# Second selection over 80 candidate sums instead of 256, and one table block issued ahead of the gate products

## The chip, the cores and the metric

The kernel runs on one core of one Trainium2 chip. The metric is the device time of one execution in microseconds (us); smaller is better. Each engine of the core has its own instruction queue: PE (TensorE, matrix products; PEld is its weight load), DVE (VectorE), ACT (ScalarE), POOL (GpSimd) and SP (SyncE, which here only issues loads). A queue is served in order.

## What is computed

The reference runs two transformer-like blocks over 256 tokens of width 1024. The change lies in the retrieval layer of the first block. For every token and each of 8 heads it scores 128 + 128 sub-keys, keeps the best 16 of each half, adds them pairwise, and keeps the best 16 of the 256 sums; the chosen pairs address 128 x 128 experts.

```python
s = jnp.einsum('thpk,hpnk->thpn', q, sub_keys)
sv, si = lax.top_k(s, P_TOPK)                                  # 16 of 128, two halves
cand = (sv[:, :, 0, :, None] + sv[:, :, 1, None, :]).reshape(TOKEN_BLOCK, P_HEADS, 256)
cidx = (si[:, :, 0, :, None] * N_KEYS + si[:, :, 1, None, :]).reshape(TOKEN_BLOCK, P_HEADS, 256)
fv, fpos = lax.top_k(cand, P_TOPK)                             # 16 of 256
eidx = jnp.take_along_axis(cidx, fpos, axis=-1)
g = jax.nn.softmax(fv, axis=-1)
u = u_tab[eidx]
act = jax.nn.gelu(jnp.einsum('td,thkd->thk', xb, u))
return jnp.einsum('thk,thkd->td', g * act, v_tab[eidx])
```

## The kernel before

**Every expert is computed.** The kernel does not gather rows. It multiplies all tokens by all 128 blocks of `peer_u` (128 experts each, function `U(b)`), applies gelu, multiplies by a gate matrix that is zero for experts not chosen, and multiplies by all 128 blocks of `peer_v`. One such block is 24 matrix products of 128x128 by 128x256: every weight is split into a high and a low part (`whi` by ACT, line 109; `wlo` by DVE, line 117), and `mm3` (lines 160 to 162) adds high-high, high-low and low-high. `fill` makes these parts ahead of their use, `wlo` three units ahead of the one that is issued, in the order of a fixed list of units; the raw weights come two units per load from SP (line 93), into three buffers, each free when both its units' `wlo` are made. A unit's product lands in one of two PSUM banks (`m`), which ACT empties (gelu at line 790, or a copy of a query at line 841).

**Selection, lines 806 to 850.** For head 0 to 7 the queue order is two query units, a table block, the eight score products (line 810), another table block. `tick` advances generators between units. Generator `topk` has three steps: the score products; `top16` over 128 scores, twice for each of two token halves (`tt`); the sums `cand` (line 825) and `top16` over them. `top16` (lines 308 to 319) is `max` (8 best), `max_index`, `match_replace`, `max`, `max_index`; the profile shows each `max_index` and `match_replace` as two instructions, a short MATCH_VALUE_LOAD and the pass itself. Its instructions alternate between the two halves. One head's sums are selected one unit after its scores are.

**Decoding, lines 857 to 911 (`finish`).** The position 0 to 255 of a chosen sum is split into its two ranks by a shift and a mask (lines 867, 868) and converted (line 870). Then come the softmax over the 16 (`g`, `gz`), transposes on PE (lines 881, 889), and 16 passes that turn ranks into key numbers (line 903). Two table blocks are issued between the first part of `finish` and the transposes.

**Gates, lines 923 to 976.** Loop `og` runs 32 times over 8 tokens each: DVE makes one-hot matrices `o` and `go` (lines 950, 951) one turn ahead, PE multiplies them (16 gate products, line 969), ACT copies the result into `stg` (line 972), and every second turn `stg` is written to a DRAM tensor `gd` (line 974, issued on ACT's queue). Each turn ends with one table block, as long as more than seven are left. After the loop seven blocks remain. The gates are read back as `gt` (line 990), `w_mult` (line 1000, DVE) multiplies them into the activations, `w_hi` (line 1007, ACT) and `w_lo` (line 1012, DVE) split them, and the products with `peer_v` begin. ACT's `w_hi` for blocks 0 to 2 stands in its queue between the gelus of the last blocks.

Of the kernel before, what the change touches and what calls it, by code (L numbers as in the profile page):

```python
# [13 lines left out]
F32 = mybir.dt.float32  # L14
# [6 lines left out]
OP = mybir.AluOpType  # L21
# [14 lines left out]
UKEEP = 7  # L36
# [29 lines left out]
class Kx:  # L66
# [692 lines left out]
    def peer(self):  # L759
        nc, tc, a = self.nc, self.tc, self.a  # L760
# [26 lines left out]
        def U(b):  # L787
            p = self.unit("peer_u", b, h)
            acts[b] = t = actp.tile([128, T], F32, name="act")
            nc.scalar.activation(t, p, AF.Gelu)  # L790

        pre = deque(range(2, NPRE))
        with c2:
            pkt = c2a.enter_context(tc.tile_pool(name="pkt", bufs=2))
            sx = [pk.tile([128, 8, 2, 16], U32, name=f"sx{i}") for i in range(2)]
            fx = [pk.tile([128, 8, 16], U32, name=f"fx{i}") for i in range(2)]
# [9 lines left out]
            def topk(hd, qp):  # L806
                ps = [self.side(), self.side()]
                for tt in range(2):
                    for i in range(2):
                        nc.tensor.matmul(ps[tt][:, i * 128:(i + 1) * 128], qp[:, i, tt * 128:(tt + 1) * 128],  # L810
                                         keys[:, 2 * hd + i], start=i == 0, stop=True, skip_group_check=True)
                yield
                sv_ = [pkt.tile([128, 2, 16], F32, name=f"sv{i}") for i in range(2)]
                grp = []
                for tt in range(2):
                    for i in range(2):
                        w = pkt.tile([128, 128], F32, name=f"tkw{tt}{i}", bufs=1)
                        grp.append((ps[tt][:, i * 128:(i + 1) * 128], w, sv_[tt][:, i], sx[tt][:, hd, i]))
                self.top16(grp)
                yield  # L820
                grp = []
                for tt in range(2):
                    cd = pkt.tile([128, 16, 16], F32, name=f"cand{tt}", bufs=1)
                    sv = sv_[tt]
                    nc.vector.tensor_tensor(cd, sv[:, 0, :, None].to_broadcast([128, 16, 16]),
                                            sv[:, 1, None, :].to_broadcast([128, 16, 16]), op=OP.add)
                    cf = cd.rearrange("p a b -> p (a b)")
                    w = pkt.tile([128, 256], F32, name=f"cw{tt}", bufs=1)
                    grp.append((cf, w, fv[tt][:, hd], fx[tt][:, hd]))
                self.top16(grp)  # L830

            self.tasks.append(topk(0, qp0))
            for hd in range(1, 8):
                qp = pkt.tile([128, 2, T], F32, name="qp", bufs=2)
# [4 lines left out]
                for i in range(2 if hd > 1 else 0):  # L839
                    p = self.unit("w_query", 2 * hd + i, h)  # L840
# [12 lines left out]
            pft = c2.enter_context(tc.tile_pool(name="pft", bufs=2))  # L853
# [3 lines left out]
            def finish():  # L857
                g = [pf_.tile([128, 8, 16], F32, name=f"g{tt}") for tt in range(2)]
                pf = [pf_.tile([128, 2, 8, 16], F32, name=f"pf{tt}") for tt in range(2)]
                sxf = [pf_.tile([128, 2, 8, 16], F32, name=f"sxf{tt}") for tt in range(2)]  # L860
                for tt in range(2):
                    v = fv[tt]
                    nc.vector.tensor_tensor(g[tt], v, v[:, :, 0:1].to_broadcast([128, 8, 16]), op=OP.subtract)
                    nc.scalar.activation(g[tt], g[tt], AF.Exp)
                for tt in range(2):
                    pi = pft.tile([128, 2, 8, 16], U32, name="pi")
                    nc.vector.tensor_scalar(pi[:, 0], fx[tt], 4, None, op0=OP.logical_shift_right)
                    nc.vector.tensor_scalar(pi[:, 1], fx[tt], 15, None, op0=OP.bitwise_and)
                    nc.vector.tensor_copy(sxf[tt].rearrange("p s h a -> p h s a"), sx[tt])
                    nc.vector.tensor_copy(pf[tt], pi)  # L870
                for tt in range(2):
                    gz = pft.tile([128, 8], F32, name="gz")
                    nc.vector.tensor_reduce(gz, g[tt], axis=AX.X, op=OP.add)
                    nc.vector.reciprocal(gz, gz)
                    nc.vector.tensor_tensor(g[tt], g[tt], gz[:, :, None].to_broadcast([128, 8, 16]), op=OP.mult)
                for _ in range(FW):
                    yield
                for tt in range(2):
                    p = self.side()
                    for j, src in enumerate((sxf[tt][:, 0], sxf[tt][:, 1], pf[tt][:, 0], pf[tt][:, 1])):  # L880
                        nc.tensor.transpose(p[:, j * 128:(j + 1) * 128], src.rearrange("p a b -> p (a b)"),
                                            self.ident)
                    ts = slice(tt * 128, (tt + 1) * 128)
                    p = p.rearrange("p (k s t) -> p k s t", k=2, s=2)
                    nc.scalar.copy(sxT[:, :, ts], p[:, 0])
                    nc.scalar.copy(posT[:, :, ts], p[:, 1])
                p = self.side()
                for tt in range(2):
                    nc.tensor.transpose(p[:, tt * 128:(tt + 1) * 128], g[tt].rearrange("p a b -> p (a b)"),
                                        self.ident)  # L890
                slot = pf_.tile([128, T], F32, name="slot")
                nc.scalar.mul(slot, p[:, :T], GSCALE)
                yield
                acc = self.bank(0)
                last = None
                for a0 in range(0, 16, FA):
                    cur = []
                    for a in range(a0, a0 + FA):
                        pb = self.side()
                        nc.tensor.matmul(pb, pick[:, a].rearrange("p h w -> p (h w)"),  # L900
                                         sxT.rearrange("p s t -> p (s t)"), start=True, stop=True)
                        t = pft.tile([128, 2 * T], BF, name="hit", bufs=2 * FA)
                        nc.vector.scalar_tensor_tensor(t, posT.rearrange("p s t -> p (s t)"), float(a), pb,
                                                       op0=OP.is_equal, op1=OP.mult)
                        cur.append((a, t))
                    yield
                    for a, t in cur:
                        nc.tensor.matmul(acc, identb, t, start=a == 0, stop=a == 15)
                nc.scalar.copy(ib.rearrange("p t j -> p j t"), acc.rearrange("p (j t) -> p j t", j=2))
                nc.vector.tensor_copy(gp[:, :, 0], slot)  # L910
                nc.vector.tensor_tensor(gp[:, :, 1], slot, gp[:, :, 0], op=OP.subtract)

            self.side_cycle = ("s", "s", "a1", "a2")
            self.tasks.append(finish())
            while self.tasks:
                self.tick()
# [6 lines left out]
        with ExitStack() as c3:  # L923
# [35 lines left out]
            for og in range(T // OG):  # L959
                o2, go = nxt  # L960
                if og + 1 < T // OG:
                    nxt = onehots(og + 1)
                if og % (TG // OG) == 0:
                    stg = pgt.tile([128, 128, TG], F32, name="stg")
                for q in range(OG // 4):
                    p = self.side().rearrange("p (t i) -> p t i", t=4)
                    for i in range(4):
                        for j in range(2):
                            nc.tensor.matmul(p[:, i], o2[:, q * 4 + i], go[:, q * 4 + i, j],  # L969
                                             start=i == 0 and j == 0, stop=j == 1, skip_group_check=True)  # L970
                    e0 = (og % (TG // OG)) * OG + q * 4
                    nc.scalar.mul(stg[:, :, e0:e0 + 4].rearrange("p i t -> p t i"), p, 1.0 / GSCALE)  # L972
                if og % (TG // OG) == TG // OG - 1:
                    nc.scalar.dma_start(gd[:, og * OG // TG], stg)
                if len(pre) > UKEEP:
                    U(pre.popleft())

        c1.close()
        banks = [self.bank(i) for i in range(4)]
# [607 lines left out]
```

## Time and profile before

| | |
|---|---|
| median of 3 runs | 1481.99 us (1478.51 to 1486.52) |
| profiled execution, its own time | 1480.42 us |
| its span, first to last instruction | 1478.7 us |
| PE busy | 1380.0 us, 93% |
| DVE busy | 1116.5 us, 76% |
| ACT busy | 767.0 us, 52% |

The profiled execution's time is 1.72 us more than its span, and 1.57 us less than the median. Busy shares are means over stages that have different limits; stages are told apart by windows of time, in us from the span's start.

### The profile page before, as it was taken

How to read it: one execution, taken by the hardware profiler on the slowest of the kernel's cores; microseconds unless marked ns; L12 is line 12 of the kernel's file. 1: busy time of each engine (PE TensorE's matmuls, PEld its weight loads, DVE VectorE, ACT ScalarE, POOL GpSimd, SP SyncE). 2: the span in 40 equal slices, each digit the busy share in tenths (PEclk: the TensorE clock that was granted, in tenths of full speed). 3: DMA queues.
4: the chain of work that ended last, by engine and by line, in shares of the span. 5: the costliest groups of instructions: out<-in, count | busy, mean ns of one | idle time of the engine just before them, and what ended most of it. 6: DMA issues, size and time to landing. Idle time of an engine off the chain costs nothing.

```text
span 1478.7 us, 27412 instructions
## 1 busy us (share of the span) xinstructions
PE 1380.0 (93%) x11208; PEld 1332.7 (90%) x11208; DVE 1116.5 (76%) x2066; ACT 767.0 (52%) x1241; POOL 119.3 (8%) x95
## 2 busy tenths in 40 slices
PE   3898988979999999999999999999979899899997
PEld 2777887978899999999999999999979789899997
DVE  7887789996799677777777766666789968765554
ACT  3545654424699754444445444444555485553442
POOL 0020020000000000000000000000148530100000
PEclk8999999998999999999999999999999999999999
DMA  9556543444577888888888867666445325445451
GB/s 378 188 202 211 199 158 115 146 141 143 180 279 283 291 313 294 311 309 310 285 291 312 303 214 243 221 235 211 148 141 170 132 99 198 144 160 197 172 189 68
DMA packets 106062, 317.31 MB, mean 215 GB/s; under 512 B 5584, under 2 KB 34640, under 8 KB 103632
## 3 DMA queue, kind: packets, MB, share of 16 engines
q1 hardware_dynamic: 65696, 250.54, 48.7%
q10 hardware_dynamic: 39408, 61.87, 11.8%
q0 software_dynamic: 832, 3.15, 0.6%
q8 instruction: 88, 1.44, 0.4%
q14 instruction: 38, 0.31, 0.1%
HBM read 297.71 MB, written 17.83 MB: 213 GB/s over the span
## 4 chain that ended last, share of the span: by engine, by line
PE 70%; DVE 23%; ACT 4%; issue 1%; DMA 1%; POOL 0%; DVEq 0%; POOLq 0%; SPq 0%; ACTq 0%
PE m L160 11%; PE m L161 11%; PE m L162 11%; PE a L161 11%; PE a L160 11%; PE a L162 11%; DVE wlo L117 5%; DVE a L1149 3%; PE s L969 2%; DVE junk L323 1%; DMA raw<-in_ada_w 1%; ACT whi L109 1%; DVE cacc L553 1%; DVE score L1108 1%; DVE mdt L291 1%
## 5 line engine op out<-in xcount | busy, mean ns | idle before, releaser
L160 PE MATMUL m<-hi,whi 128*128 128x256 f32 x1816 | 522.6, 288 | 10.3 <-DVE cacc L553 4.1
L117 DVE TENSOR_TENSOR wlo<-raw,whi 128x1024 fp32r<-128x1024 f32 x398 | 480.8, 1224 | 56.0 <-ACT whi L109 45.8
L162 PE MATMUL m<-hi,wlo 128*128 128x256 f32 x1816 | 513.2, 283 | 8.8 <-DVE wlo L117 8.7
L161 PE MATMUL m<-lo,whi 128*128 128x256 f32 x1816 | 513.0, 282 | 0.0
L109 ACT CAST whi<-raw 128x1024 fp32r<-128x1024 f32 x428 | 444.8, 1046 | 61.5 <-DMA raw<-in_peer_v 27.1
L160 PEld LDWEIGHTS m<-hi,whi 128*128 128x128 f32 x1816 | 347.4, 191 | 13.5 <-issue 4.3
L162 PEld LDWEIGHTS m<-hi,wlo 128*128 128x128 f32 x1816 | 346.4, 191 | 10.2 <-DVE wlo L117 9.9
L161 PEld LDWEIGHTS m<-lo,whi 128*128 128x128 f32 x1816 | 347.2, 191 | 0.6
L162 PE MATMUL a<-wh,wlo 128*128 128x256 f32 x1024 | 288.2, 281 | 0.0
L161 PE MATMUL a<-wl,whi 128*128 128x256 f32 x1024 | 288.2, 281 | 0.0
L160 PE MATMUL a<-wh,whi 128*128 128x256 f32 x1024 | 287.9, 281 | 0.0
L162 PEld LDWEIGHTS a<-wh,wlo 128*128 128x128 f32 x1024 | 192.9, 188 | 0.0
L161 PEld LDWEIGHTS a<-wl,whi 128*128 128x128 f32 x1024 | 192.7, 188 | 0.0
L160 PEld LDWEIGHTS a<-wh,whi 128*128 128x128 f32 x1024 | 192.6, 188 | 0.0
L1012 DVE TENSOR_TENSOR wl<-act,wh 128x256 fp32r<-128x256 f32 x128 | 54.5, 426 | 137.7 <-PE a L161 122.9
L790 ACT ACTIVATE act<-m 128x256 f32<-128x256 f32 x126 | 48.4, 384 | 165.4 <-PE m L162 165.4
L1007 ACT CAST wh<-act 128x256 fp32r<-128x256 f32 x128 | 51.9, 406 | 143.6 <-DVE act L1000 121.2
L323 DVE SCALAR_TENSOR_TENSOR junk<-mraw,silu 128x1024 bf16<-128x1024 f32 x80 | 97.6, 1220 | 7.2 <-DMA mraw<-in_ada_w 7.0
L117 POOL TENSOR_TENSOR wlo<-raw,whi 128x1024 fp32r<-128x1024 f32 x33 | 79.2, 2421 | 41.7 <-ACT whi L109 35.2
L972 ACT ACTIVATE stg<-s 128x512 f32<-128x512 f32 x64 | 64.6, 1119 | 3.3 <-PE s L969 3.2
L1000 DVE TENSOR_TENSOR act<-act,gt 128x256 f32<-128x256 f32 x128 | 53.7, 419 | 5.0 <-DMA gt<-gd 5.0
L161 PE MATMUL a<-fl,whi 128*128 128x256 f32 x176 | 49.8, 283 | 0.1
(438 smaller groups left out, 1801.8 us busy)
## 6 DMA issues: line engine op xcount, KB each, us to landing
raw<-in_peer_u SPq DMA_DIRECT2D x64, 1024.0 KB, 5.8
raw<-in_peer_v SPq DMA_DIRECT2D x64, 1024.0 KB, 5.1
mraw<-in_w_ada ACTq DMA_DIRECT2D x48, 512.0 KB, 5.5
raw<-in_w_ffn_in SPq DMA_DIRECT2D x22, 1024.0 KB, 5.1
gd<-stg ACTq DMA_DIRECT2D x16, 1024.0 KB, 6.9
gt<-gd ACTq DMA_DIRECT2D x14, 1024.0 KB, 8.0
mraw<-in_ada_w SPq DMA_DIRECT2D x24, 512.0 KB, 4.6
raw<-in_w_ffn_out SPq DMA_DIRECT2D x11, 1024.0 KB, 5.0
```

The lines of the kernel that those rows point to most:

```text
L109: self.nc.scalar.copy(t, self.raw[k])
L117: eng.tensor_tensor(t, self.raw.pop(k), h.bitcast(F32), op=OP.subtract)
L160: mm(out, w[0], x[0], start=start, stop=False, **kw)
L161: mm(out, w[0], x[1], start=False, stop=False, **kw)
L162: mm(out, w[1], x[0], start=False, stop=stop, **kw)
L323: self.nc.vector.scalar_tensor_tensor(junk, w, 0.5, self.silu_c[i], op0=OP.mult, op1=OP.mult, accum_out=self.mod[i][:, u:u + 1])
L790: nc.scalar.activation(t, p, AF.Gelu)
L972: nc.scalar.mul(stg[:, :, e0:e0 + 4].rearrange("p i t -> p t i"), p, 1.0 / GSCALE)
L1000: nc.vector.tensor_tensor(tv, tv, gv, op=OP.mult)
L1007: nc.scalar.copy(wts[b], acts[b])
L1012: nc.vector.tensor_tensor(wl, acts.pop(b), wts[b].bitcast(F32), op=OP.subtract)
L1149: nc.vector.scalar_tensor_tensor(zp, z[:, c, k:k + T], w, zp, op0=OP.mult, op1=OP.add)
```

## The change

A sum of rank a and rank b (counted from 0) can be among the best 16 only if (a+1)(b+1) is at most 16, since that many sums are at least as large. The new kernel forms 80 sums that contain all of these: a = 0 with b = 0 to 15, a = 1 to 7 with b = 0 to 7, and a = 8 to 15 with b = 0. `top16` runs over these 80. The position no longer splits by a shift and a mask alone, so `finish` has six more DVE instructions for each token half. Apart from that, in loop `og` the table block now stands ahead of the turn's gate products instead of behind them.

```diff
-                    cd = pkt.tile([128, 16, 16], F32, name=f"cand{tt}", bufs=1)
+                    cf = pkt.tile([128, 80], F32, name=f"cand{tt}", bufs=1)
                     sv = sv_[tt]
-                    nc.vector.tensor_tensor(cd, sv[:, 0, :, None].to_broadcast([128, 16, 16]),
-                                            sv[:, 1, None, :].to_broadcast([128, 16, 16]), op=OP.add)
-                    cf = cd.rearrange("p a b -> p (a b)")
-                    w = pkt.tile([128, 256], F32, name=f"cw{tt}", bufs=1)
+                    for a0, na, nb, o in ((0, 1, 16, 0), (1, 7, 8, 16), (8, 8, 1, 72)):
+                        sh = [128, na, nb]
+                        nc.vector.tensor_tensor(cf[:, o:o + na * nb].rearrange("p (a b) -> p a b", b=nb),
+                                                sv[:, 0, a0:a0 + na, None].to_broadcast(sh),
+                                                sv[:, 1, None, :nb].to_broadcast(sh), op=OP.add)
+                    w = pkt.tile([128, 80], F32, name=f"cw{tt}", bufs=1)
                     grp.append((cf, w, fv[tt][:, hd], fx[tt][:, hd]))
                 self.top16(grp)
...
                     pi = pft.tile([128, 2, 8, 16], U32, name="pi")
-                    nc.vector.tensor_scalar(pi[:, 0], fx[tt], 4, None, op0=OP.logical_shift_right)
-                    nc.vector.tensor_scalar(pi[:, 1], fx[tt], 15, None, op0=OP.bitwise_and)
+                    nc.vector.tensor_scalar(pi[:, 0], fx[tt], 3, None, op0=OP.logical_shift_right)
+                    nc.vector.tensor_scalar(pi[:, 1], fx[tt], 7, None, op0=OP.bitwise_and)
                     nc.vector.tensor_copy(sxf[tt].rearrange("p s h a -> p h s a"), sx[tt])
-                    nc.vector.tensor_copy(pf[tt], pi)
+                    rm = pft.tile([128, 2, 8, 16], F32, name="rm")
+                    nc.vector.tensor_copy(rm, pi)
+                    r, m = rm[:, 0], rm[:, 1]
+                    pa, pb = pf[tt][:, 0], pf[tt][:, 1]
+                    gm = pft.tile([128, 8, 16], F32, name="gm")
+                    nc.vector.scalar_tensor_tensor(gm, r, 9.0, m, op0=OP.is_equal, op1=OP.mult)
+                    nc.vector.tensor_scalar(pa, r, -1.0, 0.0, op0=OP.add, op1=OP.max)
+                    nc.vector.tensor_tensor(pa, pa, gm, op=OP.add)
+                    nc.vector.tensor_tensor(gm, m, gm, op=OP.subtract)
+                    nc.vector.tensor_scalar(pb, r, 1.0, 8.0, op0=OP.is_equal, op1=OP.mult)
+                    nc.vector.tensor_tensor(pb, pb, gm, op=OP.add)
...
                     stg = pgt.tile([128, 128, TG], F32, name="stg")
+                if len(pre) > UKEEP:
+                    U(pre.popleft())
                 for q in range(OG // 4):
...
                     nc.scalar.dma_start(gd[:, og * OG // TG], stg)
-                if len(pre) > UKEEP:
-                    U(pre.popleft())
```

## Rows read from the trace of the kernel before

**Rows 1.** Windows: start:end, length, busy us (instructions) by engine, PEclk, DMA share, GB/s.
```profile
225.00:322.50 97.50, 88.75 (x725) 87.05 (x726) 97.12 (x390) 39.58 (x61) 0.00 (x0) 0.98 0.41 140
381.00:387.40 6.40, 6.37 (x41) 6.32 (x41) 6.33 (x6) 2.85 (x3) 0.00 (x0) 0.56 0.00 0
387.40:391.20 3.80, 3.80 (x42) 3.75 (x42) 3.09 (x3) 3.24 (x5) 0.00 (x0) 1.00 0.52 160
```
**Rows 2.** Chain that ended last, one head and the last head: start us, us, what.
```profile
268.13 0.79 DVE sv L311 x4
268.93 1.06 DVE sx L313 x4
...
274.00 0.67 DVE cand L825 x2
274.67 0.65 DVE fv L311 x2
275.32 0.79 DVE fx L313 x2
...
278.35 3.39 DVE wlo L117 x3
281.74 0.79 DVE sv L311 x4
...
322.59 0.79 DVE sv L311 x4
```
**Rows 3.** Waits of PE, 225 to 345: us in total, times, longest us.
```profile
PE m L162 <- DVE wlo L117: 8.7, 6, 2.4
```
**Rows 4.** Timeline of PE, score products of heads 1, 3, 4 and 7.
```profile
231.36 1.05 PE L810 MATMUL s<-keys,qp 128*128 128x128 f32 x8
...
262.20 1.05 PE L810 MATMUL s<-keys,qp 128*128 128x128 f32 x8
...
274.40 1.05 PE L810 MATMUL s<-keys,qp 128*128 128x128 f32 x8
...
315.10 1.05 PE L810 MATMUL s<-keys,qp 128*128 128x128 f32 x8
```
**Rows 5.** Instructions that write tile cand: duration ns min/median/max, first and last start.
```profile
L825 DVE TENSOR_TENSOR cand<-sv x16: 417/425/433, 235.3 to 327.6; 128x256 f32<-128x256 f32 x16
```
**Rows 6.** Groups by line and form, a narrow add on DVE: busy us, mean ns.
```profile
L350 DVE TENSOR_TENSOR mod<-mod,small 128x8 f32<-128x8 f32 x2 | 0.3, 162 | 0.0
```
**Rows 7.** Timeline of DVE and PE, the decoding in finish.
```profile
332.25 0.22 DVE L868 TENSOR_SCALAR pi<-fx 128x128 uint32<-128x128 uint32 x1
...
333.71 0.29 DVE L873 TENSOR_REDUCE gz<-g 128x8 f32<-128x128 f32 x1 [0.16 <-ACT g L864]
334.03 0.20 DVE L874 RECIPROCAL gz<-gz 128x8 f32<-128x8 f32 x1
...
335.37 0.48 PE L889 MATMUL s<-ident,g 128*128 128x128 f32 x1 [0.28 <-DVE g L875]
336.56 0.58 PE L160 MATMUL m<-hi,whi 128*128 128x256 f32 x1 [0.71 <-ACT act L790]
```
**Rows 8.** Timeline of PE, gate products of the first two turns.
```profile
381.03 1.86 PE L969 MATMUL s<-go,o 128*128 128x128 f16 x16 [3.56 <-DVE go L951]
...
387.35 0.84 PE L969 MATMUL s<-go,o 128*128 128x128 f16 x12
```
**Rows 9.** Timeline of ACT, DVE and PE after the gate loop.
```profile
510.79 0.39 ACT L790 ACTIVATE act<-m 128x256 f32<-128x256 f32 x1 [1.51 <-PE m L162]
...
513.62 0.39 ACT L790 ACTIVATE act<-m 128x256 f32<-128x256 f32 x1 [1.51 <-PE m L162]
...
518.37 0.43 DVE L1000 TENSOR_TENSOR act<-act,gt 128x256 f32<-128x256 f32 x1 [5.00 <-DMA gt<-gd]
520.15 0.38 ACT L790 ACTIVATE act<-m 128x256 f32<-128x256 f32 x1
527.55 0.28 PE L160 MATMUL a<-wh,whi 128*128 128x256 f32 x1
```

## The prediction, made before the changed kernel was run

> **What bounds the kernel now.** I looked at the page's slices first (PE nearly full almost everywhere), then cut the stages that the diff touches into windows, and read the chain of waits and the timelines inside them.
>
> Selection, 225 to 322.5 us: DVE is busy 97.12 of 97.50 us, PE 88.75 [rows 1]. The chain runs through DVE alone: one head after the other repeats with 281.74 - 268.13 = 13.61 us [rows 2]. Of this the selection over sums takes 278.35 - 274.00 = 4.35, four `wlo` 4 x 1.13 = 4.52 (three are 3.39), and the first selection the remaining 4.74. PE waits six times, 8.7 us in all, always for `wlo` [rows 3], so for DVE's queue. The gelus 510.79 and 513.62 put a block at 2.83 us [rows 9]; a head on PE is four such units and the score products, and between heads 3 and 4 (score products at 262.20 and 274.40 us [rows 4]), where PE did not wait, it took 12.2. So DVE sets this stage, with PE 1.4 us a head behind it.
>
> Decoding: behind the last selection PE has only transposes until its next block at 336.56 [rows 7]. The wait that ends last is for a gelu (0.71), which freed a PSUM bank; the last transposes of `g` ended at 335.85, the DVE work for them being made after the conversions.
>
> [...]
>
> **The change part by part.**
>
> *Second selection.* One pass's price is its distance to the next one. `max` over 128 costs 0.79/4 = 0.198 us, over 256 0.65/2 = 0.327 [rows 2]: 1.0 ns per element. At 80 that is 0.15. Finding or replacing costs 1.06/4 = 0.265 at 128 and 0.79/2 = 0.395 at 256; at 80, 0.215. The one add costs 0.67/2 = 0.335 though its own duration is 0.425 [rows 5]: its successor starts 0.09 before it ends. A narrow add of 8 lasts 0.162 [rows 6]; with the slope (0.425 - 0.162)/248 the three adds last 0.17, 0.21 and 0.16, and cost 0.08, 0.12 and 0.07 if the overlap stays. Both halves: adds 0.55, four `max` 0.60, six others 1.29, together 2.44 instead of 4.35. Saved: 1.91 a head. A result is read by the instruction after next at the earliest; at 80 two passes of `max` take 0.30, and a result is there after 0.15 + 0.09 and the 0.03 that L874 started behind L873's end [rows 7], so it is just in time.
>
> [...]
>
> DVE never idles in this stage, so seven savings move the last head's first selection from 322.59 to 309.2, if PE has its scores ready. Head 1's were issued at 231.36 [rows 4]; six heads of 12.2 later is 304.6, plus 0.9 for the products themselves. The waits for `wlo` are at most 2.4 each [rows 3], and every `wlo` comes 1.9 earlier for each selection in front of it, while PE comes earlier only by waits already saved; adding up both queues piece by piece from 228 us with the prices above (before the change this gives 322.5 for the last head, as the row has it) leaves two waits, 0.6 and 0.8, near heads 2 and 3: ready at 306.9, 2.3 ahead of DVE. DVE's new period of 11.7 undercuts PE's 12.2: at head 1 the scores are ready 6.6 us before DVE takes them up (232.3 against 238.9), at head 7 the 2.3 are left, so the lead lasts the eight heads. The eighth saving is at the end: 8 x 1.91 = 15.3. Loads follow `wlo` and come earlier with it.
>
> *Decoding.* Per half: the cast is now waited for (0.32, the distance L873 to L874, instead of 0.20), then three adds or products of 128 at 0.20 (as two `max` of 128), two of them behind a `tensor_scalar` of 0.22 + 0.03 that they must wait for, and the subtraction at 0.20: 0.12 + 4 x 0.20 + 2 x 0.25 = 1.42, both 2.84. Low bound, no waits and `tensor_scalar` at 0.13 (L868's duration less the overlap): 2.1. High bound, every one waited for: 3.8. DVE's queue holds behind them the softmax, whose wait of 0.16 is swallowed, then three `wlo` and the key-number passes; PE waits for the transposes, which had 0.71 to spare before the gelu [rows 7]. Cost: 2.84 - 0.16 - 0.71 = 2.0 (1.3 to 2.9). The `wlo` behind are for blocks beyond the next one, and have a block's time to spare.
>
> *Moved block, start.* Now PE has a block at 377.47 (381.03 - 3.56), with weights made three ahead and a free bank. It ends at 380.30, the products start at 381.03, as `go` is where it was, and with no long standstill I take the full clock: 0.97 (3.80 - 2.83), done by 382.0 instead of 387.35 [rows 8]. Gain 5.4. Between old and new place PE's queue has the 16 products, ACT's two copies and every second turn the write of `gd`; DVE's, SP's and POOL's have nothing, so loads and one-hots keep their order. From there on a turn repeats the same cycle shifted, PE-bound at 3.80.
>
> *Moved block, end.* The last products, the last `gd` write and the read of `gt` come one block later against the remaining blocks: 2.83. `w_mult` would start at 521.2 instead of 518.37. ACT's `w_hi` waits for it, and behind it in ACT's queue is the gelu at 520.15 that frees the bank for the block after next. That block starts at 527.55 - 2 x 2.83 = 521.9 [rows 9], the gelu ends at 520.5: 1.4 to spare. Cost 2.83 - 1.4 = 1.5, between 0 (the transfers come faster) and 2.8 (the slack is gone).
>
> Sum: 15.3 - 2.0 + 5.4 - 1.5 = 17.2. From the profiled execution's own 1480.4 this gives 1463.2; from the median, 1.6 higher, 1464.8. I say 1464.
>
> **The rivals.**
>
> *Narrow passes have a floor.* No row shows a pass under 128. If 80 costs as 128 and each add 0.20, the stage takes 1.2 + 0.79 + 6 x 0.265 = 3.58, saving 0.77 x 8 = 6.2; with the decoding at 2.9, 6.2 - 2.9 + 3.9 = 7.2: 1473. For it: nothing but the gap in the rows; against it, the slope, and the add of 8 at 0.162.
>
> *The overlap is lost.* If narrow instructions each cost their duration, 0.09 more, the stage takes 1.09 + 0.96 + 1.83 = 3.88, saving 0.47 x 8 = 3.8; less 2.9, plus 3.9: 4.8, so 1475.6, within half a per cent. The passes in rows 2 overlap, which speaks against it. [...]
>
> *The start gives back less.* If the clock falls in spite of the shorter standstill, only the block's 2.83 is gained there, and with the whole 2.83 lost at the end the move is worth nothing: 15.3 - 2.0 = 13.3, 1467. In selection PE waited six times, up to 2.4 us [rows 3], and the mean clock there is 0.98 [rows 1], which speaks against it.
>
> *Slower: `gt` comes late.* ACT stands at `w_hi`, PE soon after. Beyond 1.4 us of slack each us costs one. The move alone uses 2.8; to eat the 18.7 gained elsewhere, `gt` would have to land some 20 us after 518.37. It decides from there. DVE's wait for it was 5.0 [rows 9]; nothing in the diff adds a transfer, and the delay would have to be four times that wait.
>
> **How the numbers follow.** Forecast 0.75, floor 0.08, lost overlap 0.06, weaker start 0.08, late `gt` 0.03. A measurement tells about 0.5%, 7.4 us, from no change. Faster: forecast, start, and half the floor's cases, 0.86; same 0.11; slower 0.03. Range: downward the best ends (no loss at the end, 1.5, decoding 0.7 cheaper, and a median 3 lower than the likeliest as the runs before spread by 3.5 to 4.5) to 1458; upward the floor's 1473.
>
> **What would show it.** The chain in selection: `cand` to the next `wlo` in 2.4 us, heads 11.7 apart, score products close in front of each first selection, the last one at 309. `finish` longer by 2.8 and PE's next block 13 us earlier than before. No standstill over 1 us before the first gate products, and a full clock after them. After the loop a wait of PE of about 1.5 for a gelu. Wrong it would be through passes that do not shrink below 128, through a PE that becomes the bound in the heads, or through a long wait at `gt`.

## The result, and the profile after

The changed kernel takes 1461.92 us in the median of 6 runs (1459.22 to 1466.49), the kernel before 1479.45 in 6 (1476.10 to 1486.52): 17.5 us less, ratio 0.9886, interval 0.9871 to 0.9902. The prediction was 1464, with 17.2 us gained. A later group of runs on another chip gave 1461.22 against 1477.57, ratio 0.9887 (0.9873 to 0.9901). The profiled execution took the longest of the first six, 1466.49 with a span of 1464.8; a wait that can account for the difference is found below.

Selection. Windows of the kernel after; the first answers to the first of [rows 1].

```profile
225.00:309.50 84.50, 83.95 (x707) 83.08 (x708) 84.12 (x420) 38.84 (x60) 0.00 (x0) 1.00 0.47 163
503.00:507.00 4.00, 0.42 (x3) 0.40 (x3) 2.08 (x4) 1.65 (x3) 0.00 (x0) 0.87 1.02 320
507.00:510.00 3.00, 3.00 (x16) 3.00 (x16) 3.00 (x5) 2.73 (x5) 0.00 (x0) 0.50 0.46 187
```

PE and DVE are both full in the stage now, 83.95 and 84.12 of 84.50 us, where PE had 8.75 us to spare. The chain that ended last, one head and the start of the last, answers to [rows 2]:

```profile
285.73 0.79 DVE sv L311 x4
...
291.60 0.58 DVE cand L827 x6
292.18 0.29 DVE fv L311 x2
292.46 0.42 DVE fx L313 x2
292.89 0.42 DVE cw L315 x2
...
293.95 3.48 DVE wlo L117 x3
297.42 0.79 DVE sv L311 x4
...
309.12 0.79 DVE sv L311 x4
```

From the sums to the next `wlo` it is 293.95 - 291.60 = 2.35 us where it was 4.35, from head to head 297.42 - 285.73 = 11.69 where it was 13.61, and the last head begins its first selection at 309.12 instead of 322.59. The wait of PE for `wlo` in this stage, 8.7 us in [rows 3], is down to this, and the last scores are ready at 305.59 + 1.05 = 306.64, 2.5 us ahead of DVE (waits, then timeline of PE):

```profile
PE m L162 <- DVE wlo L117: 0.5, 1, 0.5
```

```profile
305.59 1.05 PE L810 MATMUL s<-keys,qp 128*128 128x128 f32 x8
```

Decoding. Timeline of DVE, the conversion and the six new instructions of one token half, and the start of the next half:

```profile
317.19 0.28 DVE L873 CAST rm<-pi 128x256 f32<-128x256 uint32 x1
317.51 0.29 DVE L877 SCALAR_TENSOR_TENSOR gm<-rm 128x128 f32<-128x128 f32 x1
317.72 0.22 DVE L878 TENSOR_SCALAR pf<-rm 128x128 f32<-128x128 f32 x1
317.98 0.29 DVE L879 TENSOR_TENSOR pf<-pf,gm 128x128 f32<-128x128 f32 x1
318.30 0.29 DVE L880 TENSOR_TENSOR gm<-rm,gm 128x128 f32<-128x128 f32 x1
318.51 0.22 DVE L881 TENSOR_SCALAR pf<-rm 128x128 f32<-128x128 f32 x1
318.76 0.29 DVE L882 TENSOR_TENSOR pf<-pf,gm 128x128 f32<-128x128 f32 x1
318.97 0.22 DVE L869 TENSOR_SCALAR pi<-fx 128x128 uint32<-128x128 uint32 x1
```

Read the distances, not the durations: 0.32 where an instruction reads what the one in front of it wrote (or, as L880, overwrites what it reads), 0.20 to 0.21 where it doesn't, 0.25 to 0.26 behind a `tensor_scalar` that it needs. From the conversion to the end of the group it is 1.78 us, against the 0.20 that the conversion alone cost.

Timeline of PE: the last transposes of the gates and the block behind them, the first two turns of the gate loop, the block that waits behind the loop, and the first product with `peer_v`. They answer to [rows 7 to 9].

```profile
322.88 0.48 PE L901 MATMUL s<-ident,g 128*128 128x128 f32 x1 [0.28 <-DVE g L887]
323.01 0.56 PE L160 MATMUL m<-hi,whi 128*128 128x256 f32 x1
...
367.37 1.05 PE L983 MATMUL s<-go,o 128*128 128x128 f16 x16 [0.74 <-DVE go L963]
371.14 1.07 PE L983 MATMUL s<-go,o 128*128 128x128 f16 x16
...
506.61 0.58 PE L160 MATMUL m<-hi,whi 128*128 128x256 f32 x1 [3.58 <-ACT act L790]
...
515.14 0.28 PE L160 MATMUL a<-wh,whi 128*128 128x256 f32 x1
```

PE's next block after the selection starts at 323.01 instead of 336.56, 13.55 us earlier. Before the first gate products PE waits 0.74 us instead of 3.56, and the first turn runs at full clock (1.00 from 367.37 to 371.14): 371.14 is 3.77 behind 367.37. A block and its products are through at 371.14 - 2.83 = 368.3, against 387.35 before: 19.0 us earlier. But the first product with `peer_v` comes at 515.14, only 12.4 us earlier than 527.55. So 6.6 us were lost in between, at the wait of 3.58. Timeline of ACT and DVE there:

```profile
487.59 0.33 ACTq L988 DMA_DIRECT2D gd<-stg  x1
...
497.41 0.39 ACT L790 ACTIVATE act<-m 128x256 f32<-128x256 f32 x1 [1.50 <-PE m L162]
...
504.40 0.43 DVE L1012 TENSOR_TENSOR act<-act,gt 128x256 f32<-128x256 f32 x1 [10.06 <-DMA gt<-gd]
504.90 0.40 ACT L1019 CAST wh<-act 128x256 fp32r<-128x256 f32 x1 [7.11 <-DVE act L1012]
506.18 0.38 ACT L790 ACTIVATE act<-m 128x256 f32<-128x256 f32 x1
```

ACT stands 7.11 us at `w_hi` for the gates, and the gelu behind it, which frees PE's bank, runs at 506.18. The way from the issue of the last `gd` write to the gates' first use is 504.40 - 487.59 = 16.8 us. PE then runs at the lower clock (0.50 from 507 to 510, the third window above): two blocks take 515.14 - 506.61 = 8.53 us instead of 5.66. That is 3.58 + 2.87 = 6.45 of the 6.6.

### The profile page after: what moved, and what is told of

Its sections match the earlier page's. It is cut to its first block, busy times and chain, and to the rows that moved or that the text cites. A ratio compares the mean times of both kernels' runs of the same rounds, so it can differ in the third digit from the quotient of the medians.

```text
span 1464.8 us, 27457 instructions
## 1 busy us (share of the span) xinstructions
PE 1376.8 (94%) x11208; PEld 1329.5 (91%) x11208; DVE 1103.8 (75%) x2110; ACT 768.5 (52%) x1241; POOL 119.5 (8%) x95
## 4 chain that ended last, share of the span: by engine, by line
PE 72%; DVE 20%; ACT 4%; DMA 2%; issue 1%; POOL 0%; POOLq 0%; DVEq 0%; SPq 0%; ACTq 0%
PE m L160 12%; PE m L162 12%; PE m L161 12%; PE a L160 11%; PE a L162 11%; PE a L161 11%; DVE wlo L117 4%; DVE a L1161 3%; PE s L983 2%; DVE junk L323 2%; ACT whi L109 1%; DMA raw<-in_ada_w 1%; DVE cacc L553 1%; DMA gt<-gd 1%; DVE mdt L291 1%
## 5 line engine op out<-in xcount | busy, mean ns | idle before, releaser
L217 POOL TENSOR_TENSOR act<-act 128x256 f32<-128x256 f32 x7 | 5.6, 801 | 551.5 <-ACT act L208 551.1
```

## The experiments

Each time stands against the kernel before in the same group of runs.

**One part alone.** `sel_only` is the changed kernel with the block put back behind the gate products; `move_only` is the kernel before with only this edit:

```diff
                     stg = pgt.tile([128, 128, TG], F32, name="stg")
+                if len(pre) > UKEEP:
+                    U(pre.popleft())
...
                     nc.scalar.dma_start(gd[:, og * OG // TG], stg)
-                if len(pre) > UKEEP:
-                    U(pre.popleft())
```

> The selection over 80 sums with its decoding; the table block of each turn stays behind the gate products as before. Theory (the two parts add up, and each works where the prediction put it): the last head's first selection starts near 309 us, the decoding costs 2.0, PE waits 3.5 us for the first one-hots and runs the first turn at the lower clock, and there is no wait of PE over 1 us after the gate loop: 13.3 us less than before. Rival (the end of the gate loop is short of cover in any faster kernel, whatever the order inside the loop, because the gates are read back late): a PE wait of 2 to 4 us after the gate loop here too, and 8 to 10 us less than before.

> The selection over 256 sums as before; only the table block of each turn stands ahead of the gate products. Theory: 5.4 us gained before the first gate products (standstill 0.7 instead of 3.6, full clock behind it), and between 1.5 (my prediction) and 6.6 us (what the profile of the changed kernel shows) lost after the loop, where PE waits for a gelu that stands behind the gates' arrival: 4 us less than before down to 1 us more. Rival (the move is free at the end, and the wait in the changed kernel comes from something else): 5 us less, no wait of PE after the loop.

`sel_only` took 1465.49 us against 1478.86, 13.4 less (ratio 0.9911, 0.9897 to 0.9925), `move_only` 1475.94, 2.9 less (0.9978, 0.9968 to 0.9988). Together 16.3, beside 17.5 and 16.4 for both at once: the parts add up within what the intervals tell. Waits of PE, 225 to 560, in `sel_only` and in `move_only`:

```profile
PE s L981 <- DVE go L963: 3.6, 1, 3.6
```

```profile
PE m L160 <- ACT act L790: 2.4, 2, 1.7
PE s L971 <- DVE go L951: 0.7, 1, 0.7
```

Without the move there is the standstill at the start and no wait for a gelu behind the loop; with it the start's is 0.7 and the end's 1.7 (the other 0.7 of the 2.4 is the one of [rows 7]). The rival that any faster kernel runs short of cover there falls with the profile of `sel_only`.

**The decoding.** `nodecode` writes the conversion straight into `pf`, in place of the conversion and the six instructions:

```diff
-                    rm = pft.tile([128, 2, 8, 16], F32, name="rm")
-                    nc.vector.tensor_copy(rm, pi)
...
-                    nc.vector.tensor_tensor(pb, pb, gm, op=OP.add)
+                    nc.vector.tensor_copy(pf[tt], pi)
```

> The changed kernel without the six extra instructions per token half that turn a position among 80 into two ranks: it takes shift and mask as ranks, so the experts' gates go to wrong places. Theory: the extra instructions cost 2.0 us, as the transposes of the gates then end 2.8 earlier and the next table block waits for a gelu instead: 2 us less than the changed kernel, about 19 less than before. Rival (they are hidden behind the exponentials and table loads of ACT): no difference to the changed kernel.

It took 1460.59, 18.3 less than before (0.9875, 0.9857 to 0.9892); these runs don't tell that from the changed kernel. The trace does. Timeline of PE in `nodecode`, the block behind the transposes:

```profile
320.53 0.58 PE L160 MATMUL m<-hi,whi 128*128 128x256 f32 x1 [0.71 <-ACT act L790]
```

It comes 4.48 us after ACT began to load its table for the exponentials (316.05), in the changed kernel 323.01 - 316.68 = 6.33 after. So the six instructions cost 1.85 us, and without them the gelu ends the wait, as it did before. `late_pf` keeps them, but puts them behind the softmax in DVE's queue and the transposes of the ranks one block later in PE's:

```diff
                     nc.vector.tensor_copy(sxf[tt].rearrange("p s h a -> p h s a"), sx[tt])
+                    pis.append(pi)
+                for tt in range(2):
+                    gz = pft.tile([128, 8], F32, name="gz")
...
+                for tt in range(2):
+                    pi = pis[tt]
                     rm = pft.tile([128, 2, 8, 16], F32, name="rm")
...
-                    for j, src in enumerate((sxf[tt][:, 0], sxf[tt][:, 1], pf[tt][:, 0], pf[tt][:, 1])):
+                    for j in range(2):
...
                 yield
+                for tt in range(2):
+                    p = self.side()
+                    for j in range(2):
+                        nc.tensor.transpose(p[:, j * 128:(j + 1) * 128], pf[tt][:, j].rearrange("p a b -> p (a b)"),
+                                            self.ident)
```

> The changed kernel with the six extra instructions behind the softmax in DVE's queue, and the transposes of the ranks one table block later in PE's, so that nothing waits for the extra instructions before that block. Theory (they cost 1.85 us because PE's next block stands behind the transposes): that block starts about 2 us earlier after the last selection, less up to 1 us that the key-number passes then wait for the ranks: 1 to 2 us less than the changed kernel. Rival (the time is lost again at once, since the first key-number pass waits for the ranks): no difference.

Timeline of PE in `late_pf`:

```profile
322.65 0.58 PE L160 MATMUL m<-hi,whi 128*128 128x256 f32 x1 [0.71 <-ACT act L790]
```

The block starts 322.65 - 318.16 = 4.49 after the table load, 1.84 less than in the changed kernel, and the first key-number pass, counted from the first instruction on the chosen sums, 10.85 after it instead of 12.57. So the trace shows 1.7 us saved and kept to that point. The time, 1461.75 against 1478.72 (0.9872, 0.9852 to 0.9893), is not told apart from the changed kernel's 0.9887: whether it beats it is open.

**More cover behind the gate loop.** `keep8` and `keep10` are the changed kernel, `before_keep6` is the kernel before, each with one number changed:

```diff
-UKEEP = 7
+UKEEP = 8
```

> The changed kernel with eight instead of seven table blocks left for after the gate loop, so one block less before it: every gate product, and the read back of the gates, comes one block earlier against the blocks behind the loop. Theory (the end's loss is missing cover of one block): the gain before the first gate products stays, the wait of PE after the loop shrinks from 3.6 to below 1.5 us and its clock does not fall: 3 to 6 us less than the changed kernel, 20 to 23 less than before. Rival (the read back takes longer because other loads run beside it, so it moves with whatever is put there): the wait stays at 2 us or more and the time at the changed kernel's.

> The changed kernel with ten instead of seven table blocks left for after the gate loop. Theory (missing cover behind the loop costs 1 to 3 us in the median, and eight blocks had just enough of it): no wait of PE for a gelu after the loop and 1 to 3 us less than the changed kernel beside it. Rival (what a shorter wait saves is lost again behind it, since the time after the first product with the second table differs between executions by as much): no difference to the changed kernel that five rounds can tell.

> The kernel before, with six instead of seven table blocks left for after the gate loop: the end loses one block of cover as by the move, the start of the loop and the selection stay. Theory (cover): PE waits 1.5 to 4 us for a gelu after the loop, and 1.5 to 4 us more than before, since nothing is gained at the start. Rival (the end's loss comes from the order of the gelu and the copies inside the loop, not from cover): no wait and the time of before.

In the trace `keep8` and `keep10` did what was expected: no wait of PE behind the loop in either, and a first product with `peer_v` at 508.62 in `keep8` (timeline of PE), 6.5 us earlier than in the changed kernel's profile.

```profile
508.62 0.28 PE L160 MATMUL a<-wh,whi 128*128 128x256 f32 x1
```

In time there is nothing, and in that the theory of both missed: `keep8` 1461.70 against 1478.86 (0.9883, 0.9865 to 0.9901), `keep10` 1461.30 against 1477.57, beside 1461.22 of the changed kernel in the same group. `before_keep6` missed the theory on both counts: no wait behind the loop, and 1478.08 against 1477.57 (1.000, 0.9989 to 1.001). The next group of numbers says why its profiled execution, the fastest of 11 (1473.21), had no wait; why the median is no higher stays open, as only one execution was profiled.

**How long the gates are under way.**

> The changed kernel once more, on the same chip as the three below, with a new profile. Theory (the 3.6 us wait of PE for a gelu after the gate loop was one execution's long read back, 11.0 us to landing; the cost of the move at the end differs from execution to execution around the 1.5 us of the prediction): another wait than 3.6, between 0.5 and 4 us, and a median 16 to 18 us under before. Rival (the wait is a fixed property of the order): 3.6 again.

> The kernel before once more, for a second profile. Theory: again a standstill of PE of 3.5 to 3.6 us before the first gate products, no wait of PE after the gate loop, and from the issue of the last write of the gates to the first use between 12 and 15 us; whether the clock falls behind the standstill, and for how long, may differ (0 to 2.6 us lost). Rival: the slow first turn is a fixed part of the order, 2.5 us lost again.

> The moved block alone once more, for a second profile. Theory: a standstill of 0.7 us before the first gate products with a full clock, and after the loop a PE wait of 13.3 us less than the way from the issue of the last write of the gates to their first use (none where that is shorter). Rival: a wait that doesn't follow this way.

A second profile of the changed kernel waits still longer, in the waits of PE:

```profile
PE m L160 <- ACT act L790: 4.5, 1, 4.5
```

In the profile of the changed kernel the wait would be nil if the way were 16.8 - 3.6 = 13.2 us. With the same order and the same seven blocks that bound should hold in every execution. All with the moved block, the way worked out from the issue of the last `gd` write and the first `w_mult`:

| kernel | way, us | way less 13.2 | wait of PE, us |
|---|---|---|---|
| after | 16.8 | (sets the bound) | 3.6 |
| after_again | 17.7 | 4.5 | 4.5 |
| move_only | 14.9 | 1.7 | 1.7 |
| move_again | 14.7 | 1.5 | 1.4 |
| late_pf | 14.9 | 1.7 | 1.7 |
| nodecode | 14.5 | 1.3 | 1.3 |
| sums24 (below) | 14.4 | 1.2 | 1.2 |
| gt_alone (below) | 14.2 | 1.0 | 1.0 |

With the block behind the products, or one block more at the end, the bound is a block of 2.83 higher, 16.0: `before` 14.6, `before_again` 14.7, `sel_only` 15.1 and `keep8` 14.1 stay under it, and none waits. `before_keep6` has the bound 13.2 again, but a way of 11.8 in its profile. So the cover is understood, and the length of the way, 11.8 to 17.7 us, is what differs. In the kernel after, it was long in both profiled executions, and these took the longest of their groups (1466.49 and 1467.83, medians 1461.92 and 1461.22). That its other executions had a shorter way fits their times, but none of them was profiled. In an execution with 14.5 us one more block of cover would save 1.3, which these runs don't resolve.

**What makes the way long.** `gt_alone` takes the second read of the gates (1024 KB) and two loads for the modulation (512 KB each) out of the first read's neighbourhood:

```diff
-                    (nc.gpsimd if i < 2 else nc.scalar).dma_start(gt, gd[:, :, i * GI:(i + 1) * GI].rearrange("p g i t -> p g (i t)"))
+                    (nc.gpsimd if i < 1 else nc.scalar).dma_start(gt, gd[:, :, i * GI:(i + 1) * GI].rearrange("p g i t -> p g (i t)"))
...
-            gload(1)
-            self.chores.extend(self.mod_chores(seq, pv, 2, nc.scalar, nc.gpsimd))
             while len(pre) > 3:
                 U(pre.popleft())
...
+            gload(1)
+            self.chores.extend(self.mod_chores(seq, pv, 2, nc.scalar))
             for b in range(NB - 1):
```

> The changed kernel with the second read of the gates and the first two loads for the modulation taken out of GpSimd's queue and issued on ACT after the last of the seven blocks, so that only weights run beside the first read of the gates. Theory (the first read takes 7 to 11 us because 2 MB of other loads share the DMA engines with its 1 MB): the first read lands in 4 to 6 us, PE's wait for a gelu is gone, 1 to 3 us less than the changed kernel. Rival (the read's own small pieces set its length): 7 us or more to landing, the wait stays.

The theory fell: the read takes 8.8 us to landing where 4 to 6 were expected, PE still waits 1.0, and the kernel takes 1465.66, 4.4 more than the changed kernel beside it. The loads that come late now hold up PE: ACT waits 6.0 us for the first of the modulation, DVE 7.1 for ACT, and `w_lo` stands behind that in DVE's queue (waits of PE, `gt_alone`):

```profile
PE a L161 <- DVE wl L1024: 2.3, 1, 2.3
PE a L162 <- DVE wlo L117: 1.1, 1, 1.1
```

What sets the length of the way is open, but the traces show more of it. It has two parts: from the issue of the last `gd` write to the issue of the read, and from there to the first `w_mult`. These are 7.3 and 7.3 us in `before`, 5.3 to 5.4 and 9.0 to 9.5 in `move_only`, `move_again`, `late_pf`, `nodecode` and `sums24`. What goes with the second part is the next load of weights on SP's queue. It is issued 2.0 to 2.7 us behind the read in `before`, `before_again`, `sel_only`, `before_keep6` and `keep8`, whose read part takes 7.1 to 7.6; 1.3 to 1.6 behind it in those five and in `gt_alone` and `keep10`, where it takes 8.8 to 9.5; and 1.0 behind it and 0.4 ahead of it in `after` and `after_again`, where it takes 11.0 and 10.5. `gt_alone` left that load 1.4 behind the read. That this load lengthens the read is a rival that no run tests by itself.

**How near PE stands in the selection.** `sums24` forms only 24 sums:

```diff
-                    for a0, na, nb, o in ((0, 1, 16, 0), (1, 7, 8, 16), (8, 8, 1, 72)):
+                    for a0, na, nb, o in ((0, 1, 16, 0), (1, 1, 8, 16)):
```

> The changed kernel with only 24 sums in the second selection (a = 0 with all b, a = 1 with the first 8), so 56 of the 80 sums are left out and some experts are missed. At the prices of the changed kernel the selection over sums would take 1.6 instead of 2.4 us a head. Theory (PE stands close behind DVE in this stage, as its 12.2 us a head allow no more): DVE now waits for score products in the last heads, the last head's first selection begins 3.8 us earlier than in the changed kernel instead of 5.5, and the time is 4 to 5 us less. Rival (PE has room: its units run faster once no weight is late): no such wait of DVE, 6 us less.

It took 1456.19 against 1478.72 (0.9844, 0.9827 to 0.9861), 22.5 less than before, so 5.0 and 6.2 less than the changed kernel in its two groups; the time alone doesn't decide. Waits of DVE, and timeline of DVE at the last head:

```profile
DVE sv L311 <- PE s L810: 1.3, 2, 0.7
```

```profile
305.38 0.94 DVE L311 MAX8 sv<-s 128x8 f32<-128x128 f32 x4 [0.69 <-PE s L810]
```

At the last head DVE now waits 0.7 us for the scores (the other 0.6 is at the first head), and the last first selection is 3.7 us earlier than in the changed kernel, for 3.8 in the theory and 5.5 with room on PE. So PE is the bound at the last head; the theory had the wait in the last heads, and it came only there.

## Why the prediction was right

**Second selection.** Right, with its size: 2.35 us where 2.44 was predicted, 11.69 a head for 11.7, the last head at 309.12 for 309.2, the end of the last selection 15.4 us earlier (`g` at 316.31 instead of 331.70) for 15.3. The slope between the widths 128 and 256 held down to 80, and nearly to 24 (in the timeline of `sums24` a `max` takes 0.11 where the slope gives 0.09, finding 0.16 for 0.16). The rival of a floor falls with `max` at 80: from the sums to the first search, 292.46 - 291.60 = 0.86, the adds take 0.58 and two `max` 0.29, where 0.30 was expected. The rival of the lost overlap falls too: the six narrow adds take 0.58, near the 0.55 expected and not the 1.09 that their durations would need. In the decoding, too, instructions of 0.29 us start 0.21 apart where the next one doesn't need the one in front of it. One that reads what stands directly in front of it starts 0.32 us after it, behind the end of its 0.28 to 0.29, or 0.25 to 0.26 after a `tensor_scalar` of 0.22.

**PE's lead.** Right: 2.5 us ahead of DVE at the last head, 2.3 predicted, with one wait for `wlo` of 0.5 where two, of 0.6 and 0.8, were expected. `sums24` shows how much more was to be had, 3.7 us at the last head.

**Decoding.** Right: 1.85 us, shown by `nodecode`, for 2.0. Per half the group costs 1.78 - 0.20 = 1.58 more than the conversion did, a little over the 1.42, as the subtraction too waits for the add in front of it. The whole came out under 2.0 all the same, because PE had more to spare than 0.71: its block starts 323.01 - 322.88 = 0.13 after the start of the last transpose, not after the whole 0.48 of it, so before the change 336.56 - 335.37 - 0.13 = 1.06 were free.

**Moved block, start.** Right in the profiles: 19.04 - 13.67 = 5.4 us gained between the end of the last block in front of the loop (363.8 for 377.47) and the end of the first turn, as predicted. A turn at full clock takes 3.80 before (gate products at 387.35 and 391.15) and 3.77 here. What was not foreseen is that 2.5 of them depend on the execution (last section).

**Moved block, end.** The mechanism of the wait was right, the size was right in other kernels with the moved block and not in the two profiles of the changed kernel itself. Predicted was a way that stays what it was, 14.6 us, and 1.5 lost; the ways of 14.4 to 14.9 lost 1.2 to 1.7, and the two blocks behind the wait took 5.76 to 5.77 us there, near the 5.66 of two blocks at full clock. The profiled execution of the changed kernel had 16.8 and lost 6.5, with the lower clock behind the wait; the second had 17.7 and lost 4.5 in the wait and 1.6 behind it. That the way stayed near 14.6 elsewhere was luck in part: the prediction had the loads keep their order, and its sum took their times as kept too, but the move made the part up to the read's issue some 2 us shorter and the read some 2 longer, and these nearly cancel. The rival of a late `gt` is thus real in kind, and far from the 20 us at which it would decide.

**Sum.** 13.3 for the selection measured 13.4 alone; 3.9 for the move measured 2.9, interval 1.8 to 4.7; 17.2 for both measured 17.5 and 16.4. (The chances for faster add up to 0.87, not 0.86.)

## What to carry to other kernels

Price an instruction of a queue by its distance to the next one, at two widths: here the slope between 128 and 256 carried to 80 (2.35 us for 2.44). Where an instruction read what stood directly in front of it, the whole duration counted here (0.32 from one to the next at 0.28 to 0.29, against 0.20 to 0.21). Before a queue is made faster, add up the other engine's work in the same period: here 12.2 us a head on PE let DVE go from 13.6 to 11.7, and with still less to do (`sums24`) DVE waited for scores at the last head. When work is moved ahead to fill a standstill, look for what that work covered at its old place, and express the cover as a time that a transfer may take: one profile gave 13.2 us, and seven others obeyed it. A change that adds no transfer and keeps their order can still move them against each other (here 7.3 and 7.3 us became 5.3 to 5.4 and 9.0 to 9.5): compare the distances between the issues, before and after.

## What the runs showed that was not expected

The same standstill of PE, 3.56 us before the first gate products with the block behind them, was followed by three different clocks. Windows of `before_again`, `sel_only` and `before_keep6` behind it:

```profile
381.00:384.00 3.00, 3.00 (x22) 3.00 (x20) 2.97 (x4) 2.39 (x3) 0.00 (x0) 0.50 0.00 0
```

```profile
365.70:368.00 2.30, 2.23 (x24) 2.22 (x24) 2.27 (x3) 1.58 (x2) 0.00 (x0) 0.79 0.00 0
368.00:370.00 2.00, 2.00 (x11) 2.00 (x11) 2.00 (x3) 1.27 (x2) 0.00 (x0) 0.50 0.00 0
```

```profile
380.80:384.00 3.20, 3.19 (x36) 3.19 (x36) 3.17 (x3) 2.54 (x3) 0.00 (x0) 1.00 0.00 0
```

In `before_again` the first turn took 6.22 us (380.56 to 386.78), 2.4 more than in `before_keep6`, where it took 3.78 (380.81 to 384.59) at a granted clock of 1.00, with no fall at all; in `sel_only` it took 5.31 (365.77 to 371.08), the clock at 0.50 in the middle of the turn, from 368 to 370. So a gain counted from one profile's slow stretch, here 2.5 of the 5.4 us, is not there in every execution. The way of the gates through DRAM, a write of 1024 KB and a read of 1024 KB, took 11.8 to 17.7 us in kernels that make nearly the same transfers there, and with 2 MB of loads moved away from it, it still took 14.2.
